# The first feed-forward by seven products of quarters instead of eight, in a two-block kernel on one core

## The chip, the core and the metric

The kernel runs on one core of a Trainium2 chip. A core has five engines that run beside each other and wait for each other by semaphores: TensorE (PE in the profile; its weight loads are PEld), VectorE (DVE), ScalarE (ACT), GpSimd (POOL) and SyncE (SP), which here only issues DMAs. The metric is the device time of one execution in microseconds, lower is better.

## What is computed

Two transformer blocks over 1024 tokens of width 1024, in float32. The first has a sparse attention (8 heads) and a feed-forward with a causal convolution of three taps; every sublayer is modulated by vectors from a condition. The second has a windowed attention beside a linear recurrence, and a plain feed-forward.

```python
def conv_ffn(h, w_in, conv_w, conv_b, w_out):           # first block: D_FF = 2816
    u, v = jnp.split(h @ w_in, 2, axis=-1)
    u = lax.conv_general_dilated(u, conv_w[:, None, :], window_strides=(1,), padding=[(2, 0)], ...) + conv_b
    return (jax.nn.gelu(u, approximate=False) * v) @ w_out
...
        x = x + gt_m * y                                # y: attention
        h = rmsnorm(x, g_ffn[i]) * (1 + sc_f) + sh_f
        x = x + gt_f * conv_ffn(h, f_w_in[i], f_conv_w[i], f_conv_b[i], f_w_out[i])
    return rmsnorm(x, g_final)
...
        f = jnp.square(jax.nn.relu(u @ w_ff1[l])) @ w_ff2[l]   # second block: 4096
        h = h + rmsnorm_2(f, g_post_ffn[l])
```

## The kernel before

Activations lie with features on the partitions: a tile is 128 features by 1024 tokens, often handled as two halves of 512 tokens (`hs(half)`). Every float32 product is three matmuls in a rounded format (`mm3`, L219): operands are split into a high part (ScalarE, `hi`, L236) and a rest (`lo`, L239, on VectorE or GpSimd), and low x high, high x low and high x high are added up in PSUM. One such matmul is 128 x 128 weights by 512 columns.

**Slots.** All large tiles come from 49 slots of 128 x 1024 float32 (`slot`, `free`): a freed slot goes to the end of a line, a new tile takes the one at its head and waits until the last reader of its old content is done. `psum` deals out the eight PSUM banks by name.

**Order.** A scheduler orders the instructions of each engine by a simulated time; inside `manual_schedule` TensorE keeps the order of the program. That held for `ffn_last` and what follows, not for `ffn1`. All DMAs of the stages concerned are issued by SP in a fixed order, so one that waits for its data or its slot holds the later ones.

**Stages.** (1) The attention, `dsa` (L1162): for each head and each of four pairs of token blocks, logits, softmax (the scaling is L1128), transposes and values; beside it the modulation vectors are made (`mod_steps`, L398, 512 KB of weights each). (2) `dsa_out` (L1277): output projection, residual `x1` in eight slots, normalization of both halves (`norm_mod`, L417). (3) `ffn1` (L1348): 22 pairs of input tiles (u and g), 8 k-tiles each, for both halves; `ffn_gate` does convolution from PSUM, gelu and product; after every two tiles `ffn_out` (L1376) adds their part of the output to `x1`. Between these, `weight_sums` (L2023) makes sums of quarters of the *second* feed-forward's weights on GpSimd and writes them to memory, 32 times, four additions each. (4) The second block, from `between` (L1407) and `second` (L1895). (5) The second feed-forward, which already uses seven products of quarters: a *lead* (`lead`, L2065) with the two products that need token half 0 only, whose result is kept in memory (`early`), then five products a tile (`ffn2_in`, L2094) and, in `ffn2_out`, seven passes over 16 steps that read stored quarters (`hs`) and sums (`ts`).

Seven products: with A and B cut into 2 x 2 quarters, the four quarters of A B come from seven products of quarters or of sums of quarters, where the plain way needs eight; the rest are additions.

## Time and profile before

| | |
|---|---|
| runs of the kernel before, us | 2332.87, 2335.44, 2339.22 (median 2335.44) |
| the profiled execution, us | 2336.68 |
| its span in the profile, us | 2334.8 |
| mean granted TensorE clock, share of full | 0.965 |
| busy TensorE / VectorE / ScalarE / GpSimd | 93% / 60% / 43% / 36% |
| DMA | 333 MB, mean 143 GB/s |

The profile is one execution. Busy time is the time in which an engine has an instruction in work; matmuls overlap, so that a run of them is read from the chain of waits (how long so many take one after another) and not from the mean of one. PEclk is the clock that TensorE was granted, as a share of its full 2.4 GHz. "<-" stands for who ended a wait.

### The profile page before, as it was taken

What the parts mean: (1) busy time and instruction counts of PE and PEld (TensorE: products, weight loads), DVE (VectorE), ACT (ScalarE), POOL (GpSimd) and SP (SyncE); (2) the same over time, 40 slices, a digit from 0 to 9 for tenths busy, and PEclk for the clock granted to TensorE, in tenths of its full rate; (3) what the DMA queues carried; (4) which work ended last, traced back from release to release, by engine and by line L of the source; (5) the groups of instructions that cost most, each with busy time, mean ns of one, the idle gap of its engine ahead of it and who ended that gap; (6) DMA issues with size and microseconds to landing.
All of it is one profiled execution on the core that took longest, in us unless ns stands there. A gap on an engine that the chain in (4) does not pass through costs nothing.

```text
span 2334.8 us, 27926 instructions
## 1 busy us (share of the span) xinstructions
PE 2175.3 (93%) x10205; PEld 1806.9 (77%) x10205; DVE 1396.8 (60%) x2362; ACT 998.3 (43%) x1586; POOL 833.7 (36%) x500
## 2 busy tenths in 40 slices
PE   5875899998999999999999899999879999999997
PEld 4664778977888888888888777788657888888876
DVE  8889786789533333323333787785665554743475
ACT  4765566643322111212212367674455443644441
POOL 6225331055446565555422321332442444201012
PEclk8977999999999999999999999999889999999999
DMA  7001131174445455555312221124246776956671
GB/s 282 1 9 51 42 100 37 46 253 180 144 146 175 166 190 185 177 191 173 104 37 72 91 82 63 46 82 148 87 173 235 253 246 217 336 188 200 198 252 54
DMA packets 125837, 333.46 MB, mean 143 GB/s; under 512 B 14041, under 2 KB 15361, under 8 KB 125698
## 3 DMA queue, kind: packets, MB, share of 16 engines
q1 hardware_dynamic: 124544, 327.47, 41.3%
q10 hardware_dynamic: 1154, 4.20, 0.5%
q8 instruction: 80, 1.31, 0.2%
q14 instruction: 59, 0.48, 0.1%
HBM read 251.91 MB, written 79.71 MB: 142 GB/s over the span
## 4 chain that ended last, share of the span: by engine, by line
PE 70%; DVE 11%; ACT 3%; DMA 2%; issue 2%; POOL 0%; DVEq 0%; SPq 0%; ACTq 0%; POOLq 0%
PE pair L219 34%; PE bank L219 33%; DVE ada L398 1%; DMA ada<-in_ada_dram 1%; PE bank L1145 1%; DVE sq L317 1%; DVE xc L354 1%; DVE y L1128 1%; DMA early<-e 1%; DVE fa L354 1%; DVE y L1125 0%; PE bank L1785 0%; DVE pT L239 0%; DMA out_dram<-acc 0%; ACT whi L236 0%
## 5 line engine op out<-in xcount | busy, mean ns | idle before, releaser
L239 POOL TENSOR_TENSOR wlo<-wraw,whi 128x1024 fp32r<-128x1024 f32 x121 | 308.4, 2554 | 555.1 <-ACT whi L236 428.7
L219 PE MATMUL pair<-h,whi 128*128 128x512 f32 x1408 | 440.2, 393 | 3.8 <-DVE h L354 3.6
L236 ACT ACTIVATE whi<-wraw 128x1024 fp32r<-128x1024 f32 x143 | 150.3, 1057 | 448.7 <-PE bank L219 120.3
L219 PEld LDWEIGHTS pair<-h,whi 128*128 128x128 f32 x1408 | 266.2, 190 | 62.5 <-DVE h L354 7.5
L219 PE MATMUL pair<-h,wlo 128*128 128x512 f32 x704 | 275.6, 393 | 19.0 <-ACT h L236 19.0
L239 DVE TENSOR_TENSOR wl<-st,wh 128x1024 fp32r<-128x1024 f32 x112 | 141.3, 1277 | 124.7 <-ACT wh L236 68.2
L354 DVE SCALAR_TENSOR_TENSOR x<-bank,mod,x 128x512 f32<-128x512 f32 x176 | 129.9, 747 | 108.7 <-PE bank L219 104.3
L236 ACT ACTIVATE wh<-st 128x1024 fp32r<-128x1024 f32 x112 | 116.2, 1058 | 134.0 <-PE pair L219 38.7
L219 PEld LDWEIGHTS pair<-h,wlo 128*128 128x128 f32 x704 | 133.0, 189 | 48.1 <-issue 13.3
L219 PE MATMUL bank<-u,whi 128*128 128x512 f32 x448 | 141.0, 396 | 3.8 <-DVE u L239 3.8
L354 DVE SCALAR_TENSOR_TENSOR t<-pair,vec,t 128x1023 f32<-128x1023 f32 (+1 forms) x42 | 53.9, 1282 | 143.3 <-ACT t L1333 142.5
L219 PE MATMUL bank<-hl,whi 128*128 128x512 f32 x352 | 137.6, 391 | 0.8 <-DVE hl L239 0.8
L219 PE MATMUL bank<-hh,wlo 128*128 128x512 f32 x352 | 137.7, 391 | 0.0
L219 PE MATMUL bank<-hh,whi 128*128 128x512 f32 x352 | 137.3, 390 | 0.0
L219 PE MATMUL bank<-fa,wh 128*128 128x512 f32 x416 | 131.0, 397 | 0.0
L2271 POOL TENSOR_TENSOR acc<-acc,grow 128x512 f32<-128x512 f32 x16 | 24.3, 1533 | 284.6 <-ACT sq L2270 245.9
L219 PE MATMUL pair<-fa,wh 128*128 128x512 f32 x352 | 112.4, 402 | 0.0
L1341 DVE TENSOR_TENSOR t<-t,pair 128x1024 f32<-128x1024 f32 x21 | 25.7, 1222 | 145.0 <-PE pair L219 110.8
L219 PEld LDWEIGHTS bank<-u,whi 128*128 128x128 f32 x448 | 85.9, 192 | 21.9 <-DVE u L239 4.2
L219 PE MATMUL pair<-wh,wl 128*128 128x512 f32 x256 | 100.1, 391 | 2.6 <-DVE acc L2234 2.6
L219 PE MATMUL pair<-wl,wh 128*128 128x512 f32 x256 | 99.6, 389 | 0.0
L219 PE MATMUL pair<-wh 128*128 128x512 f32 x256 | 99.6, 389 | 0.0
(493 smaller groups left out, 5267.4 us busy)
## 6 DMA issues: line engine op xcount, KB each, us to landing
ada<-in_ada_dram SPq DMA_DIRECT2D x48, 512.0 KB, 6.1
st<-hs SPq DMA_DIRECT2D x96, 256.0 KB, 2.8
wraw<-in_f_in_dram SPq DMA_DIRECT2D x44, 512.0 KB, 4.4
wraw<-in_w_in_dram SPq DMA_DIRECT2D x33, 512.0 KB, 3.5
ra<-in_ff_dram SPq DMA_DIRECT2D x32, 512.0 KB, 3.8
rb<-in_ff_dram SPq DMA_DIRECT2D x32, 512.0 KB, 4.0
st<-ts SPq DMA_DIRECT2D x64, 256.0 KB, 4.2
st<-in_ff_dram SPq DMA_DIRECT2D x48, 256.0 KB, 4.3
```

Of the source, the lines that this page charges most:

```text
L219: self.nc.tensor.matmul(out, w, x, start=start, stop=stop, **k)
L236: self.nc.scalar.activation(out, src, AF.Copy, **k)
L239: (eng or self.nc.vector).tensor_tensor(out, src, hi.bitcast(F32), op=ALU.subtract)
L317: (eng or nc.vector).tensor_tensor(acc, acc, sq, op=ALU.add)
L354: (eng or self.nc.vector).scalar_tensor_tensor(out, a, s, b, op0=op0, op1=op1)
L398: nc.vector.scalar_tensor_tensor(raw, raw, 1.0, self.cond, op0=ALU.mult, op1=ALU.mult, accum_out=c)
L1128: nc.vector.tensor_scalar(y[:, :n], y[:, :n], s, None, op0=ALU.mult)
L1145: nc.tensor.transpose(ps[:, at:at + P], pr[j][:, bs(kt)], self.ident)
L1341: nc.vector.tensor_tensor(t, t, pg, op=ALU.mult)
L2271: self.nc.gpsimd.tensor_tensor(a, a, self.grow[:, hs(i)], op=ALU.mult)
```

## The change

The first feed-forward too is computed by seven products of quarters. `ffn_in`, `ffn_lead`, `ffn_gate`, `ffn_out` and `ffn_last` are gone; the second feed-forward's loops become three general ones, `seven_lead`, `seven_in` and `seven_out`, that both use.

- *Attention:* the sums of the first feed-forward's input weights (22 pairs, four GpSimd additions, two loads and three stores each) are made there, one per step from head 1 on.
- *Output projection:* only half 0 is normalized, and its tiles before the shift are kept (`n0`); the residual `x1` is written to memory (`x1d`).
- *ffn1:* `seven_lead` does 22 tiles for half 0, results to `early1`; loads run three tiles ahead, splits two, on VectorE and GpSimd in turn. Beside it `ffn1_norm` normalizes half 1 and makes the sums of activation quarters. `seven_in` does five products a tile; convolution, gelu and gate now work on SBUF tiles (`u0`, `u1`), and seven 128 x 512 pieces of each pair of gated tiles go to memory (`hs1`). The sums of the output weights are made here, one for every two tiles.
- *ffn1_out:* `x1` is loaded again; seven passes of 11 steps load a piece and a weight quarter (or sum) per step, split them and add into four banks; results go onto `x1` at the end of a pass. The second feed-forward's output-weight sums are made here, at every fourth step.
- *Second feed-forward:* its lead gets the same look-ahead, and its input-weight sums are no longer read from memory but added on VectorE when a tile is split.
- All of `ffn1` is now inside `manual_schedule`.

```diff
-SUMS_AT = {"in": 1, "out": 2}
+LEAD1_AT = (4, 7)
+NORM1_AT = (("P7", 8), ("P4", 3), ("P4", 4))
+SUMS_EACH = 4
+AHEAD_OUT1 = (7, 4)
...
-        while len(self.wraw) <= min(i + ahead_raw, len(self.wseq) - 1):
+        while len(self.wraw) <= min(i + ahead_raw, self.wstop if self.wstop else len(self.wseq) - 1):
...
+            if keep and k % 2 == 0:
+                kept.append(self.slot("n0", F32, (P, 2, HF)))
+            t = kept[-1][:, k % 2] if keep else self.scr("nt")
...
+        self.sums_setup()
+        sums = self.weight_sums(*self.t_in1)
...
+                    next(sums, None)
...
+        self.wstop = self.wat["wo", 1, KT - 1]
+        self.x1d = self.tc.dram_tile([KT, P, S], F32, name="x1d")
...
+            self.out_tile(1, m)
+            self.nc.sync.dma_start(self.x1d[m], x1[m])
...
+    def ffn1_norm(self):
...
+        acc = self.square_sums([a[:, hs(1)] for a in self.x1])[0]
+        yield
+        r = self.rstd(self.token_sums(acc), D)
+        yield
+        pb = self.bcast(r)
...
+        n0, n1 = self.n0, [self.slot("n1", F32, (P, 2, HF)) for _ in range(4)]
...
+        for k in range(KT):
+            self.stt(at(n1, k), self.x1[k][:, hs(1)], self.gsf[:, k:k + 1], pb)
+        self.free(*self.x1)
...
+        for k in range(4):
+            a, b = at(n1, k), at(n1, k + 4)
+            t, u = self.scr("sa"), self.scr("sb")
+            self.stt(t, a, d[:, k:k + 1], b, op0=ALU.add, op1=ALU.subtract)
+            fa["s1"].append(self.scaled_pack(t))
+            self.stt(u, t, sh[:, k:k + 1], at(n0, k), op0=ALU.subtract, op1=ALU.subtract)
+            fa["s2"].append(self.scaled_pack(u))
+            t = self.scr("sa")
+            self.stt(t, at(n0, k + 4), sh[:, k + 4:k + 5], u, op0=ALU.add, op1=ALU.add)
+            fa["s4"].append(self.scaled_pack(t))
+        for k in range(4):
+            t = self.scr("sa")
+            V.tensor_tensor(t, at(n0, k), at(n1, k), op=ALU.subtract)
+            fa["s3"].append(self.scaled_pack(t))
+        for k in range(4, KT):
+            pk = self.pack("fa")
...
+            nc.scalar.activation(pk[:, 0], at(n1, k), AF.Identity, bias=b, scale=1.0)
+            self.stt(pk[:, 1], at(n1, k), b, pk[:, 0].bitcast(F32), op0=ALU.add, op1=ALU.subtract)
+            fa["22"].append(pk)
+        self.free(*n0, *n1)
...
+        self.psum(f1=[0, 2, 4, 5, 6, 7], ssq=[1], rb=[3])
+        src = self.I["f_in"]
+        tile_of = lambda n: NF1 * (n % 2) + n // 2
+        norm = self.ffn1_norm()
+        next(norm)
...
+        self.seven_lead(NF1, lambda n: src[tile_of(n)], fa, lambda o, ps: nc.scalar.activation(o, ps, AF.Copy),
+                        self.early1, {a: norm for a in LEAD1_AT}, deque([nc.vector, nc.gpsimd]))
+        sums = self.weight_sums(*self.t_out1)
...
+        def load(n):
+            d = self.slot("r2", F32, (P, 2, HF))
+            raw = self.load("tb", self.t_in1[1][n][0]), self.load("tc", self.t_in1[1][n][1]), d
+            st(d[:, 0], src[tile_of(n) + NF1 // 2][:, HF:])
+            st(d[:, 1], self.early1[n][:, :HF])
+            self.u0[n] = self.slot("u0")
+            st(self.u0[n][:, :HF], self.early1[n][:, HF:])
...
+        def split(n, raw):
...
+            pk = self.pack("wd")
+            b, c = self.split_here(b), self.split_here(c)
+            self.split(pk, d[:, 0])
+            return b, c, pk, d[:, 1], [d]
...
+        def gated(n, i, a):
+            f = n // 2 + i * (NF1 // 2)
+            if n % 2 == 0:
+                t = self.h1[i] = self.slot("t")
...
+                nc.scalar.activation(t, a, AF.Identity, bias=self.v("conv_b", f), scale=w[2])
+                for s in (1, 2):
+                    self.stt(t[:, s:], a[:, :S - s], w[2 - s], t[:, s:], op1=ALU.add)
+                nc.scalar.activation(t, t, AF.Gelu)
+            else:
+                nc.vector.tensor_tensor(self.h1[i], self.h1[i], a, op=ALU.mult)
+            self.free(a)
+        def mid(n):
+            gated(n, 0, self.u0.pop(n))
+            self.mod_steps(MOD_FFN)
+            if n % 2:
                 next(sums, None)
+        def end(n):
+            gated(n, 1, self.u1.pop(n))
+            if n % 2 == 0:
+                return
+            f = n // 2
+            a, b = self.h1.pop(0), self.h1.pop(1)
+            s, v = self.slot("s"), self.slot("v")
...
+            op(s[:, lo], a[:, hi], b[:, hi])
+            op(s[:, hi], s[:, lo], a[:, lo])
+            op(v[:, lo], a[:, lo], a[:, hi])
+            op(v[:, hi], b[:, lo], s[:, hi], ALU.add)
...
+            for i, x in enumerate((a[:, lo], b[:, lo], b[:, hi], s[:, lo], s[:, hi], v[:, lo], v[:, hi])):
+                st(h[i], x)
+            self.free(a, b, s, v)
+        def before_last():
+            for _ in sums:
+                pass
+            self.out_plan(NF1 // 2, self.I["f_out"], self.t_out1[1], AHEAD_OUT1,
+                          [lambda k, i=i: self.hs1[k][i] for i in (0, 3, 1, 4, 6, 5, 2)])
+            self.make(0)
+        self.seven_in(NF1, fa, load, split, dest, mid, end, before_last)
+        self.ffn1_out()
...
+        self.x1 = [self.load("x1", self.x1d[m]) for m in range(KT)]
+        s1, z, w, u3 = ([self.slot(c, F32, (P, 2, HF)) for _ in range(2)] for c in ("s1", "z", "w", "u3"))
...
         norm = self.between(0)
+        sums = self.weight_sums(*self.t_out2)
+        def onto(a, m, hf):
+            x = self.x1[m][:, hs(hf)]
+            self.stt(x, a, self.mod[:, 40 + m:41 + m], x, op1=ALU.add)
+        def post(name, j, ps):
+            if name == "P1":
+                nc.scalar.activation(at(s1, j), ps, AF.Copy)
...
+            elif name == "P2":
+                onto(ps, j, 0)
...
+            elif name == "P3":
+                V.tensor_tensor(at(w, j), at(w, j), ps, op=ALU.add)
+                onto(at(w, j), 4 + j, 0)
+            elif name == "P7":
+                V.tensor_tensor(at(u3, j), at(s1, j), ps, op=ALU.add)
+                V.tensor_tensor(at(z, j), at(z, j), ps, op=ALU.subtract)
+                onto(at(z, j), 4 + j, 1)
+            else:
+                V.tensor_tensor(at(u3, j), at(u3, j), ps, op=ALU.add)
+                onto(at(u3, j), j, 1)
...
+        def hook(name, k):
+            if (name, k) in NORM1_AT:
...
                 next(norm, None)
...
+            if k % SUMS_EACH == 1:
+                next(sums, None)
+        self.seven_out(post, hook, True)
...
+    def seven_lead(self, N, src, fa, put, early, at, by):
+        raw, w = deque(), deque()
+        def ahead(n):
+            while len(w) + len(raw) + got[0] < min(n + 3, N):
+                raw.append(self.load("r0", src(len(w) + len(raw) + got[0])))
+            while raw and len(w) + got[0] < min(n + 2, N):
+                by.rotate(1)
+                w.append(self.split_here(raw.popleft(), by[0]))
...
+        before = None
+        for n in range(N + 1):
+            if n < N:
+                ahead(n)
+                ab, e, ps = w.popleft(), self.slot("e"), self.bank("f1")
+                got[0] += 1
+                self.prod(ps, [a[:, :HF] for a in ab], fa["11"])
+                self.nc.scalar.activation(e[:, :HF], ps, AF.Copy)
+            if before:
+                m, wb, eb, pb = before
+                self.prod(pb, [a[:, HF:] for a in wb], fa["12"], True)
+                put(eb[:, HF:], pb)
+                self.nc.sync.dma_start(early[m], eb)
+                self.free(*wb, eb)
+            before = n, ab, e, ps
+            if n in at:
+                next(at[n], None)
...
+    def seven_in(self, N, fa, load, split, dest, mid, end, before_last):
...
         self.psum(main=[0, 4, 1, 5, 2, 6, 3, 7])
         half = lambda w, i: [a[:, hs(i)] for a in w]
+        raw, parts = {}, {}
+        def ahead(n):
+            if n < N:
+                parts[n] = split(n, raw.pop(n))
+            if n + 1 < N:
+                raw[n + 1] = load(n + 1)
+        raw[0] = load(0)
+        ahead(0)
         last = None
+        for n in range(N):
+            b, c, d, s1, gone = parts.pop(n)
+            u = self.slot("u")
+            c12, c21, c22 = dest(n)
             p6, p5, p7, p4 = (self.bank("f2") for _ in range(4))
             self.prod(p6, half(b, 1), fa["s2"])
             V.tensor_tensor(u[:, :HF], s1, p6, op=ALU.add)
+            self.free(*gone)
             self.prod(p5, half(b, 0), fa["s1"])
             self.free(*b)
             if last:
                 last()
+            ahead(n + 1)
             self.prod(p7, half(c, 0), fa["s3"])
             V.tensor_tensor(u[:, HF:], u[:, :HF], p7, op=ALU.add)
+            V.tensor_tensor(c22, p5, u[:, HF:], op=ALU.subtract)
             self.prod(p4, half(c, 1), fa["22"])
             self.free(*c)
+            V.tensor_tensor(c21, u[:, HF:], p4, op=ALU.add)
+            mid(n)
+            def last(n=n, d=d, u=u, p5=p5, c12=c12):
                 self.prod(p5, (d[:, 0], d[:, 1]), fa["s4"], True)
+                V.tensor_tensor(c12, p5, u[:, :HF], op=ALU.subtract)
+                self.free(d, u)
+                end(n)
+        before_last()
...
+    def seven_out(self, post, hook, turned, late=None):
...
+        for p, (name, _, banks, on, _) in enumerate(self.plan2):
...
+            for k in range(N):
+                self.make(p * N + k + 1)
+                ab = self.w2.popleft()
...
+                step(ab, list(enumerate(banks)), k == 0, k == N - 1, on)
...
+                hook(name, k)
+            for j, ps in enumerate(banks):
...
+                post(name, j, ps)
...
+        def split(n, raw):
+            a, b = raw
+            tb, tc_ = self.slot("tb"), self.slot("tc")
+            add(tb[:, lo], a[:, lo], b[:, lo])
+            add(tb[:, hi], tb[:, lo], b[:, hi])
+            bb = self.split_here(tb)
+            add(tc_[:, lo], b[:, lo], b[:, hi])
+            add(tc_[:, hi], tb[:, hi], a[:, hi])
+            c = self.split_here(tc_)
+            self.free(a)
+            pk = self.pack("wd")
+            self.split(pk, b[:, hi])
+            self.free(b)
+            return bb, c, pk, e2[n][:, lo], []
...
     def all(self):
         self.dsa()
         self.dsa_out()
-        last = self.ffn1()
         with self.tc.manual_schedule(engines=MANUAL):
-            self.ffn_last(*last)
+            self.ffn1()
```

## Rows read from the trace of the kernel before

**Rows 1.** the page, part 1: busy time (share of the span) and instructions.

```profile
PE 2175.3 (93%) x10205; PEld 1806.9 (77%) x10205; DVE 1396.8 (60%) x2362; ACT 998.3 (43%) x1586; POOL 833.7 (36%) x500
```

**Rows 2.** stages: length, busy PE, PEld, DVE, ACT, POOL, PEclk, DMA, GB/s.

```profile
300.00:470.00 170.00, 165.21 (x1127) 149.87 (x1126) 130.09 (x298) 108.17 (x245) 28.27 (x27) 0.98 0.18 61
470.00:600.00 130.00, 119.28 (x564) 98.84 (x563) 108.97 (x143) 51.33 (x79) 68.88 (x31) 0.96 0.61 214
637.00:1240.00 603.00, 603.00 (x2662) 499.48 (x2661) 213.00 (x227) 120.75 (x114) 299.22 (x177) 1.00 0.46 153
1660.00:1793.00 133.00, 114.46 (x466) 91.66 (x466) 78.07 (x118) 67.70 (x106) 39.71 (x21) 0.91 0.50 174
1793.00:2006.00 213.00, 213.00 (x935) 176.11 (x934) 103.77 (x123) 90.35 (x107) 88.97 (x60) 0.99 0.71 241
```

**Rows 3.** chain of work, first feed-forward: start, length, what.

```profile
606.64 2.22 DVE nt L354 x4
609.28 0.75 DVE h L354
684.72 39.21 PE pair L219 x173
```

**Rows 4.** groups by shape, 637 to 1240: busy, mean ns | idle before.

```profile
L239 DVE TENSOR_TENSOR hl<-t,hh 128x1024 fp32r<-128x1024 f32 x20 | 34.8, 1741 | 34.6 <-ACT hh L236 34.6
L354 DVE SCALAR_TENSOR_TENSOR x<-bank,mod,x 128x512 f32<-128x512 f32 x144 | 106.2, 748 | 98.1 <-PE bank L219 97.6
L354 DVE SCALAR_TENSOR_TENSOR t<-pair,vec,t 128x1023 f32<-128x1023 f32 x19 | 24.4, 1283 | 126.5 <-ACT t L1333 126.5
L2026 POOL TENSOR_TENSOR rt<-ra 128x512 f32<-128x512 f32 x16 | 20.6, 1290 | 43.6 <-DMA ra<-in_ff_dram 43.6
```

**Rows 5.** tile hl: duration ns min/median/max, first and last start.

```profile
L239 DVE TENSOR_TENSOR hl<-t,hh x22: 1225/1923/2912, 635.7 to 1272.1; 128x1024 fp32r<-128x1024 f32 x22
```

**Rows 6.** timeline of GpSimd and VectorE in the attention: start, length, instruction.

```profile
402.64 2.40 POOL L239 TENSOR_TENSOR wlo<-wraw,whi 128x1024 fp32r<-128x1024 f32 x1 [28.65 <-ACT whi L236]
403.60 1.99 DVE L1128 TENSOR_SCALAR y<-y,at_s 128x1024 f32<-128x1024 f32 x1
422.55 0.76 DVE L1128 TENSOR_SCALAR y<-y,at_s 128x1024 f32<-128x1024 f32 x1
```

**Rows 7.** two stretches of the second feed-forward, columns as in rows 2.

```profile
1990.00:2030.00 40.00, 40.00 (x178) 32.90 (x177) 32.36 (x28) 27.75 (x30) 14.28 (x8) 1.00 1.03 374
1850.00:1950.00 100.00, 100.00 (x443) 82.78 (x442) 50.30 (x60) 43.00 (x53) 43.74 (x29) 1.00 0.75 253
```

**Rows 8.** line L1128 alone, 300 to 470: length, busy DVE, PEclk, DMA, GB/s.

```profile
300.00:470.00 170.00, 29.36 (x46) 0.98 0.18 61
```

**Rows 9.** timelines of TensorE and VectorE in the second feed-forward's lead.

```profile
1703.45 1.05 PE L350 MATMUL pair<-ident,ry 128*128 128x128 f32 x8
1704.62 5.36 DVE L354 SCALAR_TENSOR_TENSOR mix<-mix,vec,pair 128x512 f32<-128x512 f32 x8 [9.56 <-PE pair L350]
1741.94 1.28 DVE L1862 TENSOR_TENSOR sa<-mix,mix 128x512 f32<-128x512 f32 x2
1751.81 3.07 DVE L317 TENSOR_TENSOR sq<-sq,sq 128x512 f32<-128x512 f32 x4
```

**Rows 10.** groups by shape, 1793 to 2006, columns as in rows 4.

```profile
L239 DVE TENSOR_TENSOR wd<-r,wd 128x512 fp32r<-128x512 f32 x12 | 8.3, 693 | 17.0 <-ACT wd L236 17.0
L2122 DVE TENSOR_TENSOR u<-u,pair 128x512 f32<-128x512 f32 x16 | 11.0, 686 | 11.5 <-PE pair L219 11.3
```

**Rows 11.** chain of work in order of time, start of the second block.

```profile
1327.71 9.35 PE bank L219 x29
```

**Rows 12.** SP's waits (total, times, longest), then the chain, 1660 to 1800.

```profile
SPq L2083 <- DVE sb L354: 10.8, 1, 10.8
1738.60 10.35 issue
1751.39 8.02 PE bank L219 x24
```

477 lines of the change are left out of this document (187 added, 290 removed).

## The prediction

> **What bounds the kernel now.** I read the busy shares first: TensorE is busy 93% of the span, VectorE 60%, GpSimd 36% [rows 1]. That is an average over unlike stages, so the second view is the table of stages [rows 2]: from 637 to 1240 us, nearly all of the first feed-forward, TensorE is busy every microsecond at full clock while VectorE has 213 of 603; so is the second feed-forward's input part (1793 to 2006). Its lead (1660 to 1793) loses 18.5 us idle and runs at a mean granted clock of 0.91. The attention (300 to 470) has VectorE at 130 of 170 and GpSimd at 28. Third, the chain in order of time: it runs through TensorE alone, 39.21 us for 173 matmuls, so one 512-column matmul costs 0.2267 us [rows 3]. In this stage only fewer matmuls save time; everything else is beside them.
>
> Two side resources matter for what is added. **The port that VectorE and GpSimd share.** With GpSimd busy half of 637 to 1240, the subtraction of a split (both inputs in SBUF) takes 1.741 us on the mean against 1.225 alone, while the residual update and the convolution step, which read one input from PSUM, show 0.748 and 1.283 [rows 4, 5]. A one-input scaling from SBUF suffers too: 1.99 us beside a GpSimd subtraction, 0.76 without [rows 6]. **The DMA queue**: its best 40 us moved 374 GB/s with all 16 engines full, without a TensorE stall; a 100 us stretch runs at 253 GB/s and 0.75 [rows 7].
>
> **The change, part by part.** The profiled execution took 2336.7 us (span 2334.8), 1.2 above the median of the runs; the sum is made against it.
>
> *Removed.* The feed-forward's products are 44 x 2 x 8 x 3 = 2112 matmuls in and 22 x 2 x 8 x 3 = 1056 out, 3168. By seven products of quarters they are 22 x 24 in the lead, 22 x 60 in the rest of the input part, 7 x 11 x 12 in the output part: 2772. 396 x 0.2267 = **-89.8**. Also gone is the gap in which the first product of half 1 waited for its normalization [rows 3]; the lead needs half 0 alone: **-3.5**.
>
> *Attention: 22 weight sums* put 88 GpSimd additions of 1.29 us [rows 4], 113 us, and 22 x 2.1 = 46 MB on SP's queue into some 170 us. GpSimd goes from 28 to 141 busy, 0.83. At 0.50 a shared operation lost 0.52, so here 0.86; the 46 scalings of the probabilities [rows 8] lose 40, and VectorE goes from 130 to 170 of 170. These scalings stand ahead of TensorE's transposes, one step of attention ahead. DMA rises by 271 to 332 GB/s, below 374, so the modulation loads behind it on SP's queue come later but seldom last. Bounds 0 and, with each scaling blocked for a full 1.29, 130 + 59 - 170 = 19, plus a late load, 25. I take **+10**.
>
> *Output projection.* Eight stores of the residual, 4.2 MB, join SP's queue where it is at 0.61 of its share for 130 us [rows 2], and the prefetch of the feed-forward's weights leaves it: 0.
>
> *Lead of FFN1.* 22 x 24 matmuls, 120 us; each 5.44 us needs a load and a store of 512 KB, a split on ScalarE and alternately VectorE (1.23) and GpSimd (2.40 [rows 6]): covered, three loads and two splits ahead. What is not covered is slots. 20 of 49 are live at the start, 26 after lead 7; the normalization of half 1 then takes 4 + 20 and returns 8, so 7 free slots remain, and leads 8 and 9 use them up: the copy of lead 9 waits for the first kept tile, the split of lead 12 for the last. On VectorE the normalization is 8 x 0.67, then 36 operations of about 0.7: 31 us if nothing interferes. Its sister in the second feed-forward took from 1703.45 to 1751.81, 48 us, and reached its differences, where the first slot comes free, 38 us in [rows 9]. TensorE has five products (13.6 us) after the broadcast. With that slot at 28 us the stall is 15, with 38 it is 25 plus 4 for lead 12, with 25 it is 11. Bounds 10 and 29 (below 10 is excluded by the order in which slots come round); nearer to the shorter, since no GpSimd additions stand inside this normalization: **+16**.
>
> *Input part of FFN1*, 27.2 us per pair of tiles. VectorE: 4 splits of 1.23, 2 of 0.69, 10 evictions of 0.69 [rows 10], 4 convolution steps of 1.28, 2 gate products of 1.23: 20.8. The steps and gates now read SBUF alone, so 12 operations use the shared port. GpSimd: 4 differences and 4 additions for the output weights' sums, 8 x 1.29 = 10.3, 0.38 of the time, so 12 x 0.52 x 0.38 / 0.50 = 4.7 lost: 25.5 of 27.2. ScalarE, at 121 of 603 before [rows 2], may double and stays far from full. It holds, narrowly. Full blocking by every GpSimd operation gives 31.1: 3.9 x 11 = 43. Bounds 0 and 43, taken near the measured mean loss: **+6**. SP's queue carries 7.5 MB per pair, 276 GB/s; the stores of the seven quarters wait for GpSimd and hold the next pair's loads behind them, but those are issued a tile (13.6 us) ahead. The switches lead to input and input to output cost a few evictions each: 0 to 8, **+3**.
>
> *Output part of FFN1.* 7 passes of 11 steps, 2.72 us a step, each with one split (1.23 on VectorE) and 0.5 MB to load. That alone is 193 GB/s, as in the second feed-forward. But three sums a pass for the second feed-forward add 6.3 MB per 29.9 us, and the residual 4.2 MB comes back: the first 5 passes move 64.5 MB in 149.6 us. At 374 GB/s that needs 172.5, so +23; if the scheduler lets sums slip into the last passes, the whole part's 78 MB needs 209 of 209.5 us, so 0; at 340 GB/s it is +40. I take **+18**.
>
> The Trainium skill, DMA: Bandwidth & Descriptors, "Where 436 GB/s comes from", holds that for HBM to SBUF the HBM side, about 358 GB/s, is the limit; its table under "Measured" has 425 for one core alone. The row stands between, at 374. By estimates from that page, this part would cost about 2 at 425 and about 31 at 358, and the sum would move by -16 or +13.
>
> *Start of the second block.* Half 0 of the residual is now done two passes (60 us) before the end, so the first units' inputs are ready; before, TensorE ran 29 matmuls in 9.35 us there instead of 6.6, after a wait of 6 [rows 11]. The last four evictions of half 1 come at once instead of one a step, which gives some back. Bounds -9 and +4: **-4**.
>
> *Lead of FFN2.* 16 leads need 87.1 us and took from 1673.6 to 1792.3, 118.7. Loads stood on SP's queue behind a waiting one (10.8 us), a split came 10 us late and TensorE fell to half clock: 24 matmuls in 8.02 us instead of 5.44 [rows 12]. Now loads are issued three leads ahead and every second split leaves GpSimd. Bounds -8 and -28; what the norm's own work blocks stays: **-20**.
>
> *Input part of FFN2* adds the weights itself: 4 VectorE additions of 0.64 a tile make 9.2 of 13.6 us, and they stand before the split that TensorE waits for. Bounds 0 and, with 4 full blockings, 0.8 x 16 = 13: **+3**. Other edits (where dictionaries and tiles are made, the order of frees) change no instruction: 0.
>
> Sum: -89.8 - 3.5 - 4 - 20 + 10 + 16 + 6 + 3 + 18 + 3 = -61.3. 2336.7 - 61.3 = 2275.4, in terms of the median 2274.
>
> **Rivals.** *All of it stays covered.* Slots cost 10, the FFN2 lead returns 28, the rest nothing: 2336.7 - 89.8 - 3.5 - 4 - 28 + 10 = 2221. For it: TensorE kept 100% at 374 GB/s for 40 us [rows 7], and VectorE is far from full in most stages. Against: the attention would have to take 113 us of GpSimd for free.
>
> *The DMA queue holds less over long stretches.* At a sustained 300 GB/s the output part needs 260 us instead of 209.5 (+51, not +18) and the attention's 56 MB 188 instead of 170 (+18, not +10): 2316. For it: no row shows more than 253 for 100 us. Against: there only 0.75 was in use.
>
> *The shared port ends on the other side: slower.* If nearly every GpSimd operation blocks VectorE for its whole 1.29 us, the input part loses 43 instead of 6, the attention 19 instead of 10, the FFN1 lead 29 instead of 16, the FFN2 input 13 instead of 3, and each output pass has 13.5 + 5.5 + 14.2 = 33.2 us of VectorE against 29.9, 17 more over the sums: +86, 2361. It decides from about 70% of that blocking (61 us) on. For it: single rows show a full block [rows 6]. Against: over 603 us the mean was 0.52, four tenths of an addition. The Trainium skill, SBUF - State Buffer, "Who interferes with whom", states this as a rule: the loser of the port blocks for the whole instruction, and an instruction with two SBUF inputs is among those that need it. The rows agree on single pairs; how often they meet is what decides.
>
> That the count of matmuls would not fall is excluded by the loops.
>
> **How the numbers follow.** Forecast (2245 to 2310) 0.62; all covered 0.16; DMA 0.13; port 0.09. The range 2230 to 2325 leaves out half of the covered case, the port and the end of the DMA case: 0.20. A difference under 0.3% (7 us) can't be told from no change here. Faster: 0.62 + 0.16 + 0.07 of the DMA case = 0.85; same 0.06; slower 0.09.
>
> **What would show it.** In the profile after: TensorE 9809 instructions or a few more for the norms; the FFN1 span 670 to 680 us. Right on the lead: one gap of 10 to 25 us around lead 9, ended by VectorE's normalization. Right on the output part: a DMA share of 0.95 or more and loads of the step's tile as TensorE's releaser in the first five passes. Right on the attention: the scaling's mean time near 1.4 us. Wrong if TensorE is idle more than 30 us in the input part, or if the FFN2 lead still takes 110 us.

## The result, and the profile after

The changed kernel takes 2410.9 us (median; 2408.4 to 2415.1), the kernel before 2336.9 beside it: a ratio of 1.032, 95% interval 1.030 to 1.034. Slower by 74 us, where 61 less were forecast. The profiled execution took 2415.1 (span 2413.3).

The page of after, part 1, has the work as it was counted, 9809 TensorE instructions instead of 10205 [rows 1]:

```profile
span 2413.3 us, 28536 instructions
...
PE 2133.2 (88%) x9809; PEld 1755.7 (73%) x9809; DVE 1661.4 (69%) x2581; ACT 1098.4 (46%) x1722; POOL 900.4 (37%) x548
```

TensorE is busy 42 us less instead of 90, because some of them ran at the lower clock, and idle 121 us more. To see where, I cut each trace at the same events: the first and last copy of an attention output (`oT`), the first copy of a lead (`e`, L2144 in after), the first eviction of an input part (`u`, L2178), its last one (`y`, L2195), the last eviction of FFN1's output part (L1444). FFN1 of before has no such parts; it is counted as one, from the first copy of its products (`t`, L1327, at 602.35 us) to its last update of the residual, 719.4 us. Lengths in us, from the traces, one execution of each kernel:

```
stage                              before   after     e1     e2     e3     e4     e5
start to first oT                   269.8   264.5  267.3  265.6  268.9  270.8  270.5
attention, first to last oT         241.2   295.0  240.4  259.2  256.2  275.4  300.1
last oT to first copy of the lead    91.4    85.1   84.6   84.2   84.5   81.0   86.5
FFN1 lead                                   142.4  141.4  143.9  142.0  143.5  140.7
FFN1 input part                             337.0  299.0  301.9  314.6  333.2  333.4
FFN1 output part                            244.5  226.4  244.1  225.4  230.6  228.7
(the three together)                719.4   723.9
second block                        349.6   359.8  354.1  353.3  360.8  359.6  399.8
FFN2 lead                           120.1   116.4  114.4  115.7  115.5  116.2  103.2
FFN2 input part                     216.5   235.5  241.2  233.9  233.6  234.9  226.1
FFN2 output part, end               326.8   333.1  329.6  332.0  331.2  330.7  331.7
```

Stages that an experiment didn't touch repeat within about 3 us, but for the start (264.5 to 270.8) and the second block (353.3 to 360.8). Five stages of after with their engines, in the columns of [rows 2]:

```profile
264.00:560.00 296.00, 251.47 (x1538) 220.49 (x1538) 201.86 (x422) 149.91 (x327) 172.20 (x127) 0.91 0.68 235
645.00:787.00 142.00, 126.87 (x541) 103.76 (x542) 52.16 (x71) 56.44 (x85) 18.60 (x8) 0.94 0.46 163
787.00:1124.00 337.00, 306.40 (x1302) 248.93 (x1301) 246.62 (x239) 105.92 (x110) 151.98 (x89) 0.97 0.73 253
1124.00:1368.00 244.00, 221.13 (x952) 181.02 (x952) 165.00 (x155) 90.75 (x97) 129.95 (x70) 0.95 0.87 322
...
1845.00:2080.00 235.00, 218.68 (x939) 177.26 (x938) 164.38 (x183) 93.32 (x109) 95.94 (x60) 0.99 0.60 209
```

Except in the output part nothing is full: VectorE is at 68% in the attention and 73% in FFN1's input part, the DMA engines at 0.68 and 0.73. The losses are waits, and the lower clock behind them. In the attention they read so (waits: engine and line, what ended them; total, times, longest):

```profile
PE bank L205 <- ACT pT L222: 16.9, 7, 5.0
...
DVE pT L225 <- ACT pT L222: 40.3, 23, 6.7
...
ACT pT L222 <- DMA ta<-ra: 8.7, 5, 5.1
...
ACT pT L222 <- DMA ta<-rt: 7.2, 4, 2.3
...
ACT pT L222 <- DMA ta<-rb: 5.4, 3, 2.3
```

TensorE and VectorE wait for ScalarE's pack of probabilities (`pT`), and ScalarE waits for the *store of a weight sum* (`ta<-ra`): two things with no data in common. What joins them is the slot. A sum takes three of the 49, gives them back in program order as soon as its instructions are issued, and the next pack that comes round takes one: it can't be written until that sum's load, four additions and store are over. That was the theory to test (slots), against the port (GpSimd's additions block VectorE) and the DMA queue.

In FFN1's input part the timeline shows the port at work (start, length, engine, instruction; in brackets the idle time before and what ended it):

```profile
870.04 2.35 POOL L2088 TENSOR_TENSOR rt<-rt,rb 128x512 f32<-128x512 f32 x1
872.47 2.12 POOL L2088 TENSOR_TENSOR rb<-rt,rb 128x512 f32<-128x512 f32 x1
...
871.15 2.31 DVE L1376 TENSOR_TENSOR t<-t,u 128x1024 f32<-128x1024 f32 x1
873.39 1.74 DVE L225 TENSOR_TENSOR wd<-r,wd 128x512 fp32r<-128x512 f32 x1
875.06 0.68 DVE L2178 TENSOR_TENSOR u<-r,pair 128x512 f32<-128x512 f32 x1
...
876.37 1.22 DVE L1376 TENSOR_TENSOR t<-t,u 128x1024 f32<-128x1024 f32 x1
...
882.92 0.69 DVE L225 TENSOR_TENSOR wd<-r,wd 128x512 fp32r<-128x512 f32 x1 [5.33 <-ACT wd L222]
...
875.79 0.80 PE L205 MATMUL pair<-fa,wl 128*128 128x512 f32 x1 [2.74 <-DVE u L2178]
```

Beside two additions of GpSimd the gate product takes 2.31 us instead of 1.22 and a split 1.74 instead of 0.69; the eviction behind them comes late and TensorE waits 2.74. (The Trainium skill, SBUF — State Buffer, "Who interferes with whom", has the loser of the port blocked for the whole instruction; these two rows, longer by 1.09 and 1.05 us or most of an addition of 1.28, agree with it.) GpSimd pays too: its two additions last 2.35 and 2.12 us. This is no single case: the long gate product and the long split stand before eight of TensorE's ten waits for `u` in this stage (23.1 us in all), one in each pair of tiles from 845 to 1061 us. A little later VectorE idles 5.33 us, since the next split waits for a load. The first matmul after the wait lasts 0.80 us, one at full clock 0.39: the same products took 306.4 us of TensorE here and 296.7 without the stalls (e1 below), so in this stage the stalls are paid again, by a third, at the lower clock.

The output part is the one stage with a full resource (columns as above):

```profile
1124.00:1184.00 60.00, 46.80 (x195) 37.86 (x195) 35.72 (x22) 21.17 (x23) 33.52 (x18) 0.88 0.98 363
1184.00:1244.00 60.00, 60.00 (x267) 49.69 (x266) 39.65 (x36) 25.65 (x27) 40.62 (x23) 1.00 1.04 395
1244.00:1304.00 60.00, 56.23 (x237) 45.98 (x236) 44.59 (x32) 19.55 (x21) 41.40 (x24) 0.94 1.00 366
1304.00:1368.00 64.00, 58.10 (x259) 47.50 (x258) 45.04 (x66) 24.38 (x28) 14.41 (x7) 0.97 0.50 173
```

The DMA engines are full for 180 us. But where they move most, 395 GB/s, TensorE loses nothing: its losses lie in the first 60 us and from 1292 us on.

### The profile page after: what moved, and what is told of

Read it like the earlier page. It is cut to its first block, busy times and chain, and to the rows that moved or that the text cites. A ratio compares the mean times of both kernels' runs of the same rounds, so it can differ in the third digit from the quotient of the medians.

```text
span 2413.3 us, 28536 instructions
## 1 busy us (share of the span) xinstructions
PE 2133.2 (88%) x9809; PEld 1755.7 (73%) x9809; DVE 1661.4 (69%) x2581; ACT 1098.4 (46%) x1722; POOL 900.4 (37%) x548
## 5 line engine op out<-in xcount | busy, mean ns | idle before, releaser
L225 DVE TENSOR_TENSOR wl<-st,wh 128x1024 fp32r<-128x1024 f32 x189 | 261.0, 1404 | 193.9 <-ACT wh L222 143.4
L205 PE MATMUL pair<-fa,wh 128*128 128x512 f32 x704 | 225.7, 403 | 0.0
L225 POOL TENSOR_TENSOR wlo<-wraw,whi 128x1024 fp32r<-128x1024 f32 x54 | 139.6, 2589 | 197.8 <-ACT whi L222 132.2
L205 PE MATMUL pair<-wh,wl 128*128 128x512 f32 x432 | 172.3, 399 | 18.5 <-DVE wl L225 15.8
L205 PE MATMUL pair<-fa,wl 128*128 128x512 f32 x352 | 145.1, 412 | 44.3 <-DVE u L2178 39.4
L205 PEld LDWEIGHTS bank<-fa,wh 128*128 128x128 f32 x768 | 144.6, 188 | 30.0
L205 PEld LDWEIGHTS pair<-fa,wh 128*128 128x128 f32 x704 | 138.0, 196 | 29.0
L205 PE MATMUL bank<-fa,wl 128*128 128x512 f32 x384 | 150.3, 391 | 3.7 <-POOL wl L225 3.4
L205 PE MATMUL bank<-wh,wl 128*128 128x512 f32 x324 | 128.9, 398 | 6.4 <-DVE wl L225 6.4
L205 PE MATMUL bank<-wh 128*128 128x512 f32 x324 | 127.3, 393 | 0.0
L205 PE MATMUL bank<-wl,wh 128*128 128x512 f32 x324 | 127.2, 392 | 0.0
```

The source lines that it names most:

```text
L205: self.nc.tensor.matmul(out, w, x, start=start, stop=stop, **k)
L225: (eng or self.nc.vector).tensor_tensor(out, src, hi.bitcast(F32), op=ALU.subtract)
```

## The experiments

**What the sums cost, and by what.** e1 leaves every sum out, e2 only GpSimd's additions (the loads, the stores and the tiles that they hold stay), e3 the sums' loads and stores (its additions run on one tile, so no tiles are held either). e1 to e5 and v1 to v4 ran once each:

```diff
-        sums = self.weight_sums(*self.t_in1)      # e1, and likewise t_out1, t_out2; FFN2's input part
+        sums = iter(())                           #     splits the two loaded tiles without additions
-            add(t[:, lo], b11, b12)               # e2: the four additions go,
...
-                st(dst[0], t)
+                st(dst[0], a)                     #     the loaded tiles are stored
-        for (ra, rb), dst in zip(srcs, dsts):     # e3: one tile, loaded once
+        t = self.load("rt", srcs[0][0])
+        for _ in dsts:
+            add(t[:, lo], t[:, hi], t[:, hi])     #     four such per sum
```

> Left out: all sums of weights (in the attention, in the input part of FFN1, in its output part, and the VectorE additions in the input part of FFN2); the products that would read a sum read a plain weight tile of the same size from memory, so every product and its loads stay. This prices all side work that the sums bring, stage by stage. After took: first product of FFN1 at 642 us (before 602), input part 336, output part 247, FFN2 input 222. Theory A (the sums cause the losses, whatever the mechanism): first product near 602 to 606, input part 302 to 312, output part 210 to 215, FFN2 input 203 to 207, time about 2410.9 - 38 - 28 - 35 - 17 = 2293. Rival B (the losses come from the rest of the change: the residual's stores, the conv that now reads SBUF, the stored quarters): the first product still at 635 or later, input part 325 or more, time over 2370.

> Left out: GpSimd's additions of the weight sums alone (88 in the attention, 44 in the input part of FFN1, 64 in its output part); the loads, the slots they take and the stores stay, storing the loaded tiles. Theory port (GpSimd's additions block VectorE): the attention gives back nearly all of its 40 us (first product near 605), the input part about 25 of its 37 us. Theory slots and queue (the chain load, add, store holds slots and SP's in-order queue): the attention keeps 20 to 40 of the 40 (first product at 620 to 640), the input part keeps 20 or more. Output part: bandwidth theory 240 to 250 as in after; port theory 215 to 225. Time: port 2325, slots and bandwidth 2380.

> Left out: the loads and stores of the weight sums; as many GpSimd additions of the same shape run in the same places on one tile that is loaded once, and the products that would read sums read plain weights. Theory port: the losses stay (first product near 640, input part 325 to 336), output part 210 to 220 by bandwidth. Theory slots and queue: first product near 605 to 612, input part 305 to 315, output part 210 to 215; time about 2410.9 - 33 - 26 - 35 = 2317.

Times 2300.2, 2335.6 and 2334.5, with the kernel before at 2326.0 on that chip. In the attention the sums cost 295.0 - 240.4 = 54.6 us. Additions alone cost 15.8 (e3), traffic alone 18.8 (e2), and 20 us come only when a load, its additions and its store follow each other. Neither rival alone explains that; it is what a chain that holds slots would do. (e2 holds them too, but for a shorter time: there `pT` waits 3.1 us in all for a sum's store, against 21.3 in after.) In the input part the 38.0 us are 15.6 for additions alone, 2.9 for traffic alone, and 19.5 for both together. The output part is clean: with additions gone 244.1, with traffic gone 225.4. The rows of e1's input part, e2's output part and e3's output part:

```profile
734.00:1033.00 299.00, 296.71 (x1308) 244.98 (x1307) 216.73 (x242) 108.74 (x112) 72.30 (x40) 1.00 0.62 208
```
```profile
1055.00:1299.00 244.00, 219.49 (x964) 180.97 (x963) 137.81 (x156) 92.66 (x100) 19.63 (x11) 0.94 0.89 329
```
```profile
1066.00:1292.00 226.00, 212.35 (x939) 175.69 (x938) 152.21 (x154) 90.09 (x96) 111.46 (x70) 0.97 0.59 193
```

The 244 us of e2 come with 329 GB/s, the 226 of e3 with 193 and all additions kept: some 18 us come with the sums' loads and stores, whatever GpSimd does. That it is their bandwidth, and not the tiles that e2 holds as well, is likely from the DMA share but not shown. But 226 is still 17 above the 209.5 of its products. e1's timeline at the switch shows them (first SP's queue, then ScalarE, VectorE, TensorE):

```profile
1046.37 0.32 SPq L1400 DMA_DIRECT2D hs<-v  x1
...
1051.53 1.06 ACT L222 ACTIVATE wh<-st 128x1024 fp32r<-128x1024 f32 x1 [1.61 <-DMA hs<-v]
...
1052.62 1.22 DVE L225 TENSOR_TENSOR wl<-st,wh 128x1024 fp32r<-128x1024 f32 x1 [11.37 <-ACT wh L222]
...
1053.90 0.80 PE L205 MATMUL pair<-wh,wl 128*128 128x512 f32 x1 [11.24 <-DVE wl L225]
```

The split of the fifth step takes the slot of the last pair's quarter `v`, whose store was issued at 1046.37. My reading, which e4 tests: the slots had run out because the residual's eight loads and eight tiles of the output part were taken at once, long before their use.

Of e1, FFN2's input part (241.2) says nothing on the additions: leaving out its two tiles may have moved the splits in ScalarE's order as well; this was not followed.

**Which tile is taken when.** e4 keeps all work:

```diff
+        own = [[self.slot("ra") for _ in range(2)] for _ in range(pairs)]   # sums in place, in four tiles of their own
-LEAD1_AT = (4, 7)
+LEAD1_AT = (1, 3)
-        self.x1 = [self.load("x1", self.x1d[m]) for m in range(KT)]         # output part: at step k of P5 instead,
+            if name == "P5" and k < KT:                                     # and s1, z, w, u3 at their first use
+                self.x1.append(self.load("x1", self.x1d[k]))
```

> All work is kept; only which tile is taken when is changed, at three places. (1) The sums in the attention and in FFN1's input part work in place in four tiles of their own, so that no pack or split takes a tile that a sum's store still reads. After: first to last output transpose of the attention 295.0 us (no sums 240.4, no additions 259.2, no traffic 256.2), input part 337.0 (no sums 299.0, no additions 301.9, no traffic 314.6). Slot theory: attention 258 to 278, input part 312 to 325. Port theory: attention 288 or more, input part 330 or more. (2) The normalization of half 1 stands at leads 1 and 3 instead of 4 and 7. Slot theory: the 11.6 us gap goes, lead 126 to 132 instead of 142.4; if VectorE's normalization itself is what is late: 138 or more. (3) The residual and the output part's tiles are taken when they are needed, 14 tiles later. Slot theory: the stalls of 12.2 and 7.4 us at the switch go, output part 226 to 232 instead of 244.5; if the last pair's store and load are late in themselves: 240 or more. Time: 2345 by slots, over 2395 by the others.

2377.8 (before 2329.2). Attention 275.4: 19.6 back, the part that was neither additions nor traffic. ScalarE no longer waits there for any sum's store, and TensorE's wait for the pack falls from 16.9 us to this:

```profile
PE bank L205 <- ACT pT L222: 0.2, 1, 0.2
```

Output part 230.6: 13.9 back. For these two the slots are shown (the attention's sums also work in place, with two tiles each instead of three). Input part 333.2: only 4 back, so its loss is not the slots of the sums. The lead did not move (143.5): its gap came with the normalization, two leads after it, and even longer. After, then e4:

```profile
714.22 0.79 PE L205 MATMUL bank<-h,wl 128*128 128x512 f32 x1 [11.58 <-ACT e L2144]
```
```profile
676.80 0.79 PE L205 MATMUL bank<-h,wl 128*128 128x512 f32 x1 [15.42 <-ACT e L2177]
```

The copy `e` comes after the normalization: in ScalarE's order it stands right behind three of the normalization's splits (711.85 to 713.68 us in after), which waited for VectorE. Whether it was put there because it waits for a slot that the normalization is to free, as the prediction has it, the traces don't part from ScalarE's order alone. An earlier normalization is no cure: it does its work at once wherever it stands.

**FFN2, and the last matrix's sums elsewhere.**

```diff
-            return self.load("ra", self.I["ff1"][n]), self.load("rb", self.I["ff1"][n + NPAIR2])  # e5: and no additions
+            raw = self.load("tb", self.I["ff1"][n]), self.load("tc", self.I["ff1"][n + NPAIR2]), d
-LEAD_AT = (3, 5, 11, 12)
+LEAD_AT = (3, 5, 11, 14)
-        sums = self.weight_sums(*self.t_out2)     # in FFN1's output part
+        self.sums2 = self.weight_sums(*self.t_out2)  # one after each unit of the second block
```

> Left out: the four VectorE additions per tile in FFN2's input part; it loads two tiles and a quarter per step, as before, but plain weights (before: 203 us of work, after 235.5 from first to last eviction). If the additions and the order they force on ScalarE and VectorE cost the time: 205 to 212; if the loads one tile ahead instead of two do: 225 or more. The sums of the last matrix are all kept but made in the second block instead of in FFN1's output part: by bandwidth that part takes 225 to 230 instead of 244.5, and the second block 360 to 372 instead of 359.8, since its DMA share is 0.2 to 0.3. The last step of the normalization in FFN2's lead stands at lead 14 instead of 12: if TensorE waited there only for the squares, lead 106 to 109 instead of 116.4; if VectorE's work is the bound, 114 or more. Time: 2355 to 2375.

2422.8 (before 2329.2). FFN2's lead 103.2: in after TensorE had waited for squares that VectorE finished late (after, then e5's second block):

```profile
PE pair L309 <- DVE sq L303: 9.3, 1, 9.3
```
```profile
PE bank L205 <- POOL wlo L225: 20.8, 2, 20.5
PE pair L1480 <- POOL sq L303: 19.7, 1, 19.7
```

The sums did fit the second block's bandwidth and cost it 40 us all the same: they crowd GpSimd's queue in its first 100 us (82 busy), and the squares and splits that TensorE needs stand behind them. The expectation, made from DMA shares, was wrong. FFN2's input part took 226.1: TensorE's waits fall from the first line (after) to the second.

```profile
PE pair L205 <- DVE u L2178: 16.3, 11, 3.5
```
```profile
PE pair L205 <- DVE u L2178: 2.0, 1, 2.0
```

My 205 to 212 was made with 203, first to last `u`; by these cuts before is at 216.5. The additions, with the two tiles and the order that they bring, account for 9 of the 19 us.

**All work kept, placed otherwise.** Eight versions; all have the late tiles of e4, sums in place (those of the last matrix excepted) and the last norm step at lead 14. v1 and v2 also run the last four steps of FFN1's output part column block by column block; v2 puts the attention's additions on VectorE as well.

```diff
+        for k in range(4):
+            yield                                 # v1 on: the normalization in seven pieces, leads 1 to 8
-        sums = self.weight_sums(*self.t_in1)      # v1: 11 in the attention, 11 on VectorE in FFN1's lead
+        sums = self.ring_sums(self.t_in1[0][:11], self.t_in1[1][:11], False)
+        more = self.ring_sums(self.t_in1[0][11:], self.t_in1[1][11:], False, nc.vector)
-        sums = self.weight_sums(*self.t_out1)     # v1: on VectorE in four tiles of their own; v3: VectorE,
+        sums = self.ahead_sums(*self.t_out1, nc.vector)   # loads one sum ahead, common tiles; v4: so on GpSimd
```

> All work is kept; it is placed otherwise. Attention: 11 of the 22 sums, on GpSimd, one every second step, in four tiles of their own; with 22 so it took 275.4 us, without any 240.4: 255 to 262. Lead of FFN1: the normalization of half 1 in seven pieces at leads 1 to 8, so that a lead takes tiles between the pieces, and the other 11 sums on VectorE at leads 10 to 20. If the 11.6 us gap comes from the normalization taking its 24 tiles at once, lead 126 to 134 instead of 142.4; if it comes from VectorE's time for it, 140 or more. Input part: the sums of the output weights on VectorE instead of GpSimd. In after, 44 GpSimd additions of 1.29 us made VectorE busy 30 us longer (246.6 against 216.7), 0.68 each, as much as an addition on VectorE (0.64). Port theory: 300 to 312 instead of 337; if VectorE's throughput were the bound: 330 or more. Output part as with late tiles, 230; its last four steps go column block by column block, so the second block starts with earlier residuals: 348 to 356 instead of 359.8. FFN2's lead with the last step at 14: 103 to 109. Time about 2310, against 2329 of the kernel before there.

> As the other one, but the 11 sums of the attention on VectorE too. VectorE was busy 188 of 241 us there without sums; 44 additions of 0.64 make 216. Port theory (an addition on GpSimd costs VectorE as much as its own): attention 248 to 256, a little below the other; if VectorE's own order decides (the softmax that TensorE waits for stands behind an addition that waits for its load): 262 or more.

> All work is kept. Like the version with split sums, but the sums of the output weights in the input part, and 11 of the first sums in FFN1's lead, work in two common tiles each, with loads issued one sum ahead, and their additions stand on VectorE spread at four per pair (in the version with split sums the order of VectorE had 32 and 20 of them in a row, and one eviction waited 26.9 us behind them). Input part: 302 to 312 instead of 343 and 337, if the place of the additions on VectorE was the cause; 325 or more if VectorE's load as such is. Lead 126 to 134, attention 256 to 264, output part 228 to 236, second block 356 to 362. Time 2300 to 2315, against about 2327 of the kernel before.

> As the other one, but the additions for the output weights in the input part are on GpSimd. Their loads come a pair ahead, so that they no longer wait in GpSimd's order. Port theory: 44 additions still block VectorE 0.3 to 0.7 us each at places that TensorE waits for: input part 312 to 330, slower than the other by 8 or more. If only the late loads had made them harmful: 302 to 310.

```
stage                       v1      v2      v3      v4      v5      v6      v7      v8
attention                260.8   263.7   264.9   262.3   264.0   261.4   242.1   241.1
FFN1 lead                128.0   129.6   151.2   149.9   135.6   136.3   140.6   126.4
FFN1 input part          343.0   349.8   304.8   312.5   314.0   310.3   314.2   333.0
FFN1 output part         239.0   235.2   231.6   231.4   235.0   233.9   247.0   225.7
second block             351.7   353.7   354.9   361.5   352.8   353.0   358.7   354.9
FFN2 lead                105.8   106.5   106.3   106.0   106.4   106.2   106.0   104.5
FFN2 input part          234.4   236.5   236.7   236.4   235.7   236.5   236.0   228.7
time, us                2340.6  2357.8  2331.9  2341.1  2333.8  2329.7  2324.8  2301.1
before on that chip     2325.1  2325.1  2331.6  2331.6  2333.6  2333.6  2333.6  2335.9
```

v1's lead is the test of the gap: with the normalization in pieces 142.4 becomes 128.0, with 11 sums in it, and TensorE's one wait left there is 0.7 us. The pieces spread its tiles and its work alike. Its input part missed its 300 to 312 by far. One eviction stood behind 20 additions in VectorE's order, with little between them, some of which waited for their loads:

```profile
779.10 0.80 PE L205 MATMUL pair<-fa,wl 128*128 128x512 f32 x1 [26.87 <-DVE u L2217]
```

In v3 they stand four to a pair, with loads a pair ahead, and the input part takes 304.8; on GpSimd (v4, which differs from v3 in the engine alone) 312.5. The lead of both missed its 126 to 134 (151.2 and 149.9): there the lead's 11 sums work in common tiles, loads ahead. The row of v3's input part:

```profile
765.00:1070.00 305.00, 299.97 (x1311) 246.41 (x1310) 248.49 (x282) 110.86 (x114) 57.01 (x42) 0.99 0.79 278
```

VectorE is as busy as in after, 248.5 us against 246.6, and the stage is 32 us shorter. So VectorE's load did not make the 38 us. Nor did the additions on GpSimd as such: in v4 they stay there, and 24.5 of the 32 us come back once their loads are issued ahead; the engine is worth the other 7.7. What changed in v4 is beside which operations they fall. The gate product, which stood long before eight of the ten waits, is short again (after, then v4):

```profile
L1376 DVE TENSOR_TENSOR t<-t,u 128x1024 f32<-128x1024 f32 x21 | 36.6, 1743 | 0.4
```
```profile
L1383 DVE TENSOR_TENSOR t<-t,u 128x1024 f32<-128x1024 f32 x21 | 25.6, 1218 | 1.1
```

So the place of the additions made most of the loss; that late loads put them there is likely (GpSimd waited 7.5 us for one just before the rows shown from after). GpSimd's additions saved VectorE next to nothing in this stage: 44 of them (the trace counts 48, four of them for the next stage) made it 30 us busier in after (216.7 in e1), 0.62 to 0.68 each, and its own take 0.69 in v3:

```profile
L2152 DVE TENSOR_TENSOR ra<-ra,ra 128x512 f32<-128x512 f32 x20 | 13.7, 686 | 1.6 <-DMA ra<-in_f_out_dram 1.3
```

v2's attention (263.7) fell where VectorE's own order was to put it (262 or more) and not where the port was (248 to 256); but it lies only 3 us from v1's, so nothing is decided between the engines there.

v5 joins v1's lead, with its first sums at leads 0 and 2, and v3's input part; v6 gives the attention's sums two tiles instead of four; v7 makes the first 11 tiles' sums on VectorE in the input part and leaves the attention alone:

```diff
-        {a: more for a in range(10, 21)}                    # the lead's sums, in v1
+        {a: more for a in (0, 2, *range(9, 18))}            # in v5
+            if n < 11:                                      # v7: two raw tiles, the quarter split first,
+                self.split(pk, b[:, hi])                    # then four additions in place
+                add(a[:, lo], a[:, lo], b[:, lo])
```

> All work is kept: the input part of the version with sums ahead on VectorE (304.8 us), and the lead's 11 sums in tiles of their own as in the version with split sums (lead 128.0 instead of 151.2 with common tiles), at leads 0, 2 and 9 to 17, so that they end before the input part. If the lead's 23 us came from common tiles that its own loads waited for: lead 126 to 134, input part 302 to 308, time 2305 to 2315 against about 2330 of the kernel before, ratio 0.989 to 0.994. If it came from the sums starting earlier (traffic in the first leads), lead 140 or more and the time 2325 to 2335.

> As the placed version, but the 11 sums of the attention work in two tiles of their own instead of four, so that each waits for the one before and they spread over the attention (they were all done by 400 us of 269 to 533, and TensorE lost its time there: from 420 to 480 us, without sums, it lost none). If it is their crowding that costs: attention 250 to 257 instead of 264.0. If each addition has its price wherever it stands (24 us for 44): 260 or more. Rest as in the placed version (lead 126 to 137, input part 305 to 314): time 2315 to 2325, ratio 0.992 to 0.997.

> No sums in the attention: the first 11 tiles of FFN1's input part make theirs from two loaded tiles on VectorE, in place, and the sums of the output weights stand beside the other 11. Attention 240 to 243, as with no sums. VectorE in the input part has 19.7 us per 27.2 without sums, 24.8 with these. If additions on VectorE that wait for no store cost only their time: input part 308 to 320, time 2300 to 2312, ratio 0.985 to 0.992. If their place in VectorE's order holds TensorE up, as in FFN2's input part (some 10 us per 16 tiles more than with plain weights): input part 325 or more, time 2320 or more.

Ratios to the kernel before: v5 1.000 (0.999 to 1.001), v6 0.999 (0.997 to 1.001), v7 0.997 (0.995 to 0.999). v5 missed its 0.989: lead and input part gave 135.6 and 314.0 instead of 128 and 305; v5's lead has waits of 7.7 and 3.4 us for GpSimd's splits that v1's lacks; further it was not followed. v6's attention (261.4 where 250 to 257 was the mark of crowding) suggests that each addition has its price there, crowded or not; v7's, without any, is at 242.1, as before. v7's input part came as expected, but its time missed 2312: its lead took 140.6 and its output part 247.0.

```diff
+            if name != "P1" and k % SUMS_EACH == 1:         # v8, on v7: no sums of the last matrix in the first pass
+            pk = self.pack("wd")                            # FFN2's input part: quarter first, additions in place
+            self.split(pk, b[:, hi])
+            add(a[:, lo], a[:, lo], b[:, lo])
```

> As the version with sums on the fly, and three places changed. (1) FFN2's input part makes its sums in the same order as that version's first tiles do: the quarter that TensorE reads last is split before the additions, the additions are in place, and each half is split by itself. It took 216.5 us in the kernel before, 235.5 in after, 226.1 with plain weights. If the additions' place in the order (ahead of the split, two more tiles) costs the 10 us: 222 to 229; if the additions themselves do: 233 or more. (2) The sums of the last matrix start with the second pass of FFN1's output part, so the switch has its loads alone (404 to 406 GB/s in its first 50 us otherwise, and stalls of 10 to 13 us): output part 225 to 233 instead of 235 to 247 if the traffic causes the stalls; 238 or more if the late store and load of the last pair do. (3) The lead's sums stand at leads 10 to 20: lead 126 to 132 instead of 140.6, if the early ones were in its way. Time 2303 to 2315, ratio 0.987 to 0.993.

v8 takes 2301.1 against 2335.9, a ratio of 0.987 (0.984 to 0.989): the change, with the same products, 1.3% faster than the kernel before. All three places answered: output part 225.7, lead 126.4, FFN2's input part 228.7. How much each gives is less sure: the traced execution of v8 took 2291.3, 10 us under its median, and that of v7 2334.3, 10 over, so some 20 of the 44 us between their columns are not the edits'. In FFN2's input part the wait of TensorE for the eviction `u` is now

```profile
PE pair L205 <- DVE u L2269: 5.3, 10, 0.9
```

against 16.3 in after. So of the 9 us that come with the additions about 7 go with their order, the two tiles that they no longer take and the splits by halves. Its FFN1 input part (333.0, 314.2 in v7) pays for the lead: in VectorE's order 12 additions of the lead's last three sums (730.5 to 748.2 us) stand ahead of one eviction:

```profile
751.86 0.80 PE L205 MATMUL pair<-fa,wl 128*128 128x512 f32 x1 [12.41 <-DVE u L2269]
```

## Why the prediction was wrong, point by point

The steps that failed are the bounds of the two stages that lost most. In the attention the bound priced VectorE's throughput and the bytes, and put the slots at nothing: at most 25 us, and it lost 53.8. In FFN1's input part the term was VectorE's average time per pair with an average loss, and the wait of TensorE for one eviction was put at nothing: +6, and it lost 38.0.

Measured against its terms (after minus before, or after minus the length without the cause):

- **Products -89.8**: right in the count, 9809, and in the price where nothing stalls: e1's input part took 299.0, and 22 x 60 x 0.2267 is 299.2. With the lower clock behind its stalls TensorE's busy time fell by 42 us only.
- **The gap of the norm -3.5: misread.** The chain [rows 3] goes through VectorE there, but TensorE had products of half 0 to do meanwhile, and its wait in before was 0.5 us:

```profile
PE pair L219 <- DVE h L354: 0.5, 1, 0.5
```

- **Attention +10, bounds 0 to 25: it lost 53.8.** The failed step is the bound. I priced VectorE's throughput (a mean scaling of 1.4 us; it was 0.86, from 0.65, and VectorE was busy 202 of 296 us) and the bytes, and took DMA below 374 GB/s for harmless. I used the count of slots for the lead and forgot it here, where a sum takes three. The price has three parts, 16 for additions, 19 for traffic, 20 for the slots they hold together (e1 to e4).
- **Output projection 0**: 6.3 less by these cuts, whose end is not the same event in both kernels; a small unforeseen gain at most. That the prefetch and the splits of FFN1's weights left it is likely, but was not tested.
- **FFN1 lead +16, bounds 10 to 29: +23** (142.4 against 119.7 of products). The place was right: one gap of 11.6 us, ended by the copy of lead 9 behind the normalization; the rest are shorter waits and their half clock. v1 shows that a normalization in pieces removes it. That the copy waited for a slot is argued, not shown.
- **FFN1 input part +6, bounds 0 to 43: +38.** The step from a mean loss of 0.52 us per operation to 25.5 of 27.2 us, so that it holds narrowly, failed twice: VectorE was not at 25.5 but at 22.4 of 30.6, and an average says nothing of where a delay falls. It fell on the two operations ahead of the eviction that TensorE waits for, in nearly every pair. The rival of the port gave 43. Its full block is what those rows show; its sum, VectorE full at 31.1, is not, so that it came near is in part luck: v3 has the same VectorE load and loses 6, v4 keeps GpSimd's additions and loses 13.5.
- **Switches +3, bounds 0 to 8: 17** at the switch into the output part, of which the late tiles give 14 back (e4).
- **FFN1 output part +18: 18** (244.5 - 226.4), and this is luck. The term was five passes slowed evenly by 64.5 MB at 374 GB/s [rows 7]. The DMA share was as forecast, but passes 2 to 5 took 29.9 us each in after, as without sums (e1); the first five ended 3 us later than in e1. The 18 are these 3, 10 in the sixth pass and 5 in the seventh, the last with the DMA engines half idle. What holds the sixth was not followed.
- **Second block -4: +10**, 4 to 11 over the runs that leave it alone. I put the earlier half 0 above the four evictions that come at once at the end. The trace has an 8.2 us wait for half 1's squares on GpSimd. With the last steps column block by column block (v1) this wait was 2.5 us and the stage took 351.7, but the output part was 8.4 us longer than e4's, so nothing is won.
- **FFN2 lead -20: -3.7.** I took the loads on SP's queue for the bound; TensorE then reached the squares 9.3 us before VectorE had them. With that step two leads later, it is -14 to -17 (e5, v1 to v8).
- **FFN2 input part +3, bounds 0 to 13: +19**; 9 come with the additions (e5), and 7 of them go when order, tiles and the splits by halves change (v8); the rest was not traced.
- Start and end, not in the sum, gave -5.3 and +6.3; not looked into.

The prediction's own tests saw it: TensorE idle 30.6 us in the input part (30 was the mark), FFN2's lead at 116 (110), the scaling at 0.86 (1.4), and no load as TensorE's releaser in passes 2 to 5, where it lost nothing. Its fault as a sum was that nine stages were each priced by their busiest resource. The range left the port's case out and ended at 2325; but all upper bounds of the terms at once (25, 29, 43, 8, 40, 4, -8 and 13) give 2397 only, since each stopped at full use of an engine or queue, and a wait between two engines that are both half idle has no such bound.

## What to carry to other kernels

Before work is put beside a stage, count the buffers: a tile given back in program order behind a load, an addition and a store is not free for as long as that chain lasts, and the next to take it is whoever comes round, often the critical path. Place matters more than load: put an addition where its operands have long landed and no eviction stands behind it (v3 against after: same VectorE time, 32 us; v4: the same additions on GpSimd, with their loads ahead, 24.5). And take tiles when they are used: sixteen tiles asked for too early cost 14 us at a switch.

## What the runs showed of the hardware

- In FFN1's input part an addition on GpSimd cost VectorE nearly as much of its own time as the addition would have cost there, 0.62 to 0.68 us against 0.69. It falls on operations with both inputs in SBUF (the gate product 2.31 for 1.22), while the eviction from PSUM above kept its 0.68. It is no fixed price: in the attention the 88 additions made VectorE 14 us busier, 0.16 each (201.9 in after, 188.0 in e1).
- The DMA engines went past the 374 GB/s of before: 395 GB/s, loads and stores together, over 60 us in after, at a share of 1.04. (The Trainium skill, DMA: Bandwidth & Descriptors, "Where 436 GB/s comes from", puts HBM to SBUF at about 358; this row is above it, and nearer the 425 of its table under "Measured".)
- A stall is paid more than once: 28 us more idle in the input part than in e1, and 10 us more busy for the same products at the lower of TensorE's two clocks. In the attention 35 us more idle came with 20 more busy (e1's row; after's is above):

```profile
267.00:508.00 241.00, 231.92 (x1540) 209.04 (x1540) 187.97 (x423) 149.64 (x328) 54.19 (x39) 0.97 0.29 98
```
